# Heads' sums of squares made inside the next unit, and three turns between the load and the rotation of the first queries

## The chip, the core and the metric

One Trainium2 chip, one core. The metric is the device time of one execution in microseconds. Runs of the same kernel agree closely: the three shown lie between 1270.07 and 1270.75 us.

## The reference

One step of a hybrid decoder trunk, for a prompt of 16 meta and 512 new tokens and for 8 sample rows of one token each. All is f32.

```
h = rmsnorm(x) @ w_in;  q, k, v, z_a, u, z_s, g_a, g_s = split(h)
q, k = rope(rmsnorm per head (q, k))          # 16 q heads, 4 kv heads, 64 wide
o_a = sink_attention(q, k, v)                 # window of 128 in blocks of 128, 16 meta keys, one sink per head
      (sample rows: against caches of 16 + 128 keys per row)
y_s = s5_branch(u)                            # diagonal state-space scan, gelu, y * sigmoid(y @ w_glu + b)
out = x + (sigmoid(g_a) * ((o_a * silu(z_a)) @ w_attn_out)
         + sigmoid(g_s) * ((y_s * silu(z_s)) @ w_ssm_out)) @ w_out
```

The per-head rmsnorm needs the sum of squares of each head of q and k: these are "the heads' sums". The kernel also returns the new windows and states.

## The kernel before, in words

**Tiles and units.** Activations lie transposed: features on the 128 partitions, 520 token columns (or 536, with the meta columns) in two column halves of 260 (or 268). Every f32 product is made of three matmuls with split operands (hi x hi, lo x hi, hi x lo). A *unit* is one block of 128 output features: `mm` (L1117) runs over 16 (in later stages 8) blocks of 128 input features and, for each, 3 x 2 matmuls; with 16 that is 96 matmuls in two halves of 48, and ws.get() fetches the weights of each half (`raw` is loaded by SP's queue, ACT makes `whi` at L971, DVE makes `wlo` at L972). After every 24 matmuls `mm` gives the background one step.

**The background** (`Background`, L927) holds three lanes of generators. Each step has a budget; a generator is run until its yielded costs use it up. `yield None` ends its turn for this step. While `fair` is off, as in the attention stage, the first lane that has work is served first and the others get what is left of the step when it yields None.

**Stages.** Some 13 groups of four units in a cheaper scheme ("quads") end at about 374 us. Then the list `ORDER1` runs u units (input of the state-space branch), h units (q, k and v heads) and x units one by one, with the state-space work in the background. Attention follows in the background of the remaining x units (loop at L1616, until nx is 47, and one last unit at L1624 to L1640), of the 8 units of Y1 (the state-space gate) and of the 16 units of Y2. `bg.drain()` (L1670) runs whatever is left, then come the 16 units with A (w_attn_out) and the last quads with w_out.

**Heads' sums.** `heads(i)` (L1283) makes one h unit, scales it and sends it to DRAM. ACT squares it (L1298). Every second unit that is not v closes with four matmuls (L1307) which sum the squares over the 64 features of a head: the stationary operand `k_sel` is 32 columns wide, and the four write four groups of 32 partitions. ACT copies the result (L1310) and two DMAs on SP's queue bring it to skD (k) or sqD (q), L1314. After the last h unit (n is 11) `head_norms()` (L1316) loads these sums, makes inverse roots on DVE and stores them, and the generator `samples()` (sample heads) joins lane 2.

**Attention.** In the generator `attention()` (L1545), values and keys come first, then the sample's attention joins lane 1 (`sample`, L841): 16 pieces of the k cache, each loaded on POOL's queue into one of two `cache` buffers, multiplied with q (L859) and summed (L860) on DVE, later the same for v (L875, L876). Lane 0 goes on with the queries: `load_q` loads raw q rows and their norms on SP's queue, `queries` rotates them on DVE (L650 to L659) and splits them (L727), `blocks` then runs five steps for each of four blocks: `scores` (L743, L744 on PE into the one `aux` bank pair; ACT copies to S, L747; DVE lays the previous block in by a mask, L749), `softmax` (DVE L755, L756, L761, L766; ACT exponentials L759, Pn L765), `turn` (transposes L774, L775; `po` on DVE L778, `pm` and `pp` on ACT L780, L784), `weigh` (L792, DVE L797 into oT). When lanes are empty, `attended` splits oT into A (ACT L1599, DVE L1600), eight pieces.

```
        at.load_q(0)
        yield None
        for kv in range(4):
            yield from at.queries(kv)
            if kv == 0:
                for _ in range(NDELAY):
                    yield None
            yield from at.blocks(kv, kv == 3)
```

Of the kernel before, what the change touches and what calls it, by code (L numbers as in the profile page):

```python
# [897 lines left out]
GBUDGET = 0.4  # L898
BUDGET2, BUDGET3, BUDGET4 = 5.6, 3.0, 4.6
HIGH = 4000  # L900
NDELAY = 2
ATTC = (("kg", 1), ("kgs", 1), ("qg", 1), ("qgs", 1), ("mown", P), ("mprev", P), ("bd64", 4), ("sink", 16))
NXR = 10
# [49 lines left out]
class Stream:  # L953
# [20 lines left out]
    def make(self, i):  # L974
        with self.tc.high_priority(offset=HIGH):
            self.piece(i, self.tiles(i), slice(0, 8))
# [12 lines left out]
class Quads:  # L989
# [29 lines left out]
    def make(self, r):  # L1019
# [9 lines left out]
        lo = pool.tile([P, 8, P], F32R, name="wlo", bufs=bufs)  # L1029
        with self.tc.high_priority(offset=HIGH):  # L1030
            for oi in self.SUMS[s]:
# [20 lines left out]
def trunk(tc, A, O):  # L1052
# [11 lines left out]
    bg = Background(tc)  # L1064
# [34 lines left out]
    def xkeep(kt, src, c):  # L1099
# [14 lines left out]
            v.scalar_tensor_tensor(out=l, in0=s, scalar=g, in1=h.bitcast(F32), op0=ALU.mult, op1=ALU.subtract)  # L1114
        yield

    def mm(n, hi_of, lo_of, w0, budget=None, after=None, pool=None, name=None):  # L1117

        ps = pool.tile([P, 2, 512], F32, name=name) if pool else mmp.tile([P, 2, 512], F32, name="mm")
        W = CH - w0  # L1120
        for h in range(n):
            wh, wl = ws.get()
            for k in range(8):
                kt = 8 * h + k
                first, last = kt == 0, kt == 8 * n - 1
                for (wt, xo, f, l) in ((wh, hi_of, first, False), (wh, lo_of, False, False), (wl, hi_of, False, last)):
                    for c in range(2):
                        m = nc.tensor.matmul(ps[:, c, 0:W], lhsT=wt[:, k], rhs=xo(kt, c), start=f, stop=l)  # L1128
                if k % 4 == 3:
                    bg.last = m.ins  # L1130
                    bg.after = (ws.dve,) if at is not None else ()
                    bg.step((bud[0] if budget is None else budget) / 2)
            if after:
                after(h)
        return ps[:, :, 0:W]
# [147 lines left out]
    def heads(i):  # L1283

        W = CH if i < 4 else 260
        ps = mm_x(CH - W)
        sb = ev.tile([P, 2, W], F32, name="z")
        with tc.high_priority(offset=HIGH):
            v.tensor_tensor(out=sb, in0=ps, in1=R_[:, :, CH - W:], op=ALU.mult)
        nc.sync.dma_start(out=rawD[i][0][:, :, CH - W:], in_=sb)  # L1290
        if i in (2, 3):
            nc.sync.dma_start(out=O["v"][i - 2], in_=sb)
            return
        for q in range(4):
            b = 32 * (q ^ 1)
            nc.sync.dma_start(out=rawD[i][1][b:b + 32, :, CH - W:], in_=sb[32 * q:32 * q + 32])
        sq = ev.tile([P, 2, W], F32, name="t")
        nc.scalar.activation(out=sq, in_=sb, func=AF.Square)  # L1298
        sqs.append(sq)
        if i % 2:  # L1300
            if "ax" not in S:
                S["ax"] = aux.tile([P, 2, 512], F32, name="aux")
            ps = S["ax"][:, 1, P:]
            for c in range(2):
                for j in range(2):
                    o = 64 * j + 32 * c
                    nc.tensor.matmul(ps[o:o + 32, 0:W], lhsT=C["sel"], rhs=sqs[j][:, c], start=True, stop=True)  # L1307
            sqs.clear()
            ss = ev.tile([P, W], F32, name="z")
            nc.scalar.copy(out=ss, in_=ps[:, 0:W])  # L1310
            dst = skD if i < 4 else sqD[2 * (i - 5):2 * (i - 5) + 4]
            dst = dst.rearrange("(j h) (c w) -> j c h w", j=2, c=2)
            for j in range(2):
                nc.sync.dma_start(out=dst[j], in_=ss[64 * j:64 * j + 64:16])  # L1314

    def head_norms():  # L1316
        for src, dst, p, n in ((skD, rkD, 67, 32), (sqD, rqD, P, 65)):
            r1 = ev.tile([p, n], F32, name="z")
            r2 = ev.tile([p, n], F32, name="z")
            flat2 = lambda t: t.rearrange("a b -> (a b)").rearrange("(p n) -> p n", n=n)  # L1320
            nc.sync.dma_start(out=r1, in_=flat2(src))
            v.tensor_scalar(out=r1, in0=r1, scalar1=1.0 / 64, scalar2=1e-6, op0=ALU.mult, op1=ALU.add)
            rsqrt_dve(nc, ev, r2, r1, [p, n], "t", "")
            nc.sync.dma_start(out=flat2(dst), in_=r2)
# [3 lines left out]
    def samples():  # L1328
        smp.extend((yield from sample_heads(nc, sp, dram, smc, C["idn"], rawD, rkD, rqD, S["ax"][:, 1, P:],
                                            lambda: tc.issue_after(bg.last))))  # L1330
# [169 lines left out]
    for n_, (kind, n) in enumerate(ORDER1):  # L1500
# [4 lines left out]
        if kind == "h":  # L1505
            heads(n)
            if n == 11:
                head_norms()
                bg.add(samples(), lane=2)
            continue  # L1510
        if sp is None:
            spool = tc.tile_pool(name="ssm", bufs=2, side="right")
# [25 lines left out]
    def attention():  # L1538
# [32 lines left out]
        at.load_q(0)  # L1571
        yield None
        for kv in range(4):
            yield from at.queries(kv)
            if kv == 0:
                for _ in range(NDELAY):
                    yield None
            yield from at.blocks(kv, kv == 3)
# [313 lines left out]
```

## Time and profile before

| | us |
|---|---|
| runs | 1270.07, 1270.47, 1270.75 (median 1270.47) |
| profiled execution: its time | 1270.79 |
| its span (first to last instruction) | 1268.7 |
| busy: PE | 1257.2 (99%) |
| busy: DVE | 962.5 (76%) |
| busy: ACT | 621.9 (49%) |
| busy: POOL | 262.1 (21%) |
| granted clock of PE, mean | 0.998 |

PE is the engine that sets the time in nearly every stage, so one reads this profile from PE's few gaps: the list of what PE waited for, and the timeline of PE, where each main matmul of 260 columns starts 0.12 us after the one before it. The distance between two starts above that is lost. The other engines matter where PE waits for them. The line numbers are those of the kernel before; in the changed kernel the lines behind the edits stand 1 to 11 lower down (L1128 becomes L1132, L1307 becomes L1313, L1599 and L1600 become L1610 and L1611).

### The profile page before, as it was taken

How to read it: one execution, taken by the hardware profiler on the slowest of the kernel's cores; microseconds unless marked ns; L12 is line 12 of the kernel's file. 1: busy time of each engine (PE TensorE's matmuls, PEld its weight loads, DVE VectorE, ACT ScalarE, POOL GpSimd, SP SyncE). 2: the span in 40 equal slices, each digit the busy share in tenths (PEclk: the TensorE clock that was granted, in tenths of full speed). 3: DMA queues.
4: the chain of work that ended last, by engine and by line, in shares of the span. 5: the costliest groups of instructions: out<-in, count | busy, mean ns of one | idle time of the engine just before them, and what ended most of it. 6: DMA issues, size and time to landing. Idle time of an engine off the chain costs nothing.

```text
span 1268.7 us, 26523 instructions
## 1 busy us (share of the span) xinstructions
PE 1257.2 (99%) x10405; PEld 1231.7 (97%) x10405; DVE 962.5 (76%) x1535; ACT 621.9 (49%) x1330; POOL 262.1 (21%) x434
## 2 busy tenths in 40 slices
PE   9999999999999999999999999999999999999998
PEld 9999999999999999999999999899899999999998
DVE  8686878887785676887668668899876567787875
ACT  8554454454458655445532233576666433344342
POOL 0003999930002222022214131211100000000000
PEclk9999999999999999999999999999999999999999
DMA  8544343353447654555554499677854555565441
GB/s 292 205 160 154 124 142 119 133 168 131 146 133 230 182 163 137 168 164 163 154 151 120 137 283 277 211 239 228 266 167 151 187 183 185 158 202 156 150 138 52
DMA packets 107905, 219.13 MB, mean 173 GB/s; under 512 B 21884, under 2 KB 47444, under 8 KB 107748
## 3 DMA queue, kind: packets, MB, share of 16 engines
q1 hardware_dynamic: 99172, 198.53, 48.8%
q0 software_dynamic: 8608, 18.90, 5.7%
q8 instruction: 82, 1.34, 0.4%
q14 instruction: 43, 0.35, 0.1%
HBM read 181.50 MB, written 36.79 MB: 172 GB/s over the span
## 4 chain that ended last, share of the span: by engine, by line
PE 86%; issue 5%; DMA 4%; DVE 2%; ACT 1%; SPq 1%; POOL 1%; DVEq 0%; POOLq 0%; ACTq 0%
PE mm L1128 44%; PE pr L1335 32%; PE wg L792 2%; DMA xr<-in_x 1%; PE aux L1335 1%; PE aux L1128 1%; PE mm L1637 1%; PE tr L526 1%; PE wg L526 1%; PE aux L743 1%; DMA cache<-in_kc 1%; PE aux L744 1%; PE tr L774 1%; DMA qv<-qD 0%; PE tr L469 0%
## 5 line engine op out<-in xcount | busy, mean ns | idle before, releaser
L1038 DVE TENSOR_TENSOR wlo<-raw,whi 128x1024 fp32r<-128x1024 f32 x147 | 181.7, 1256 | 61.1 <-ACT whi L1037 59.0
L1037 ACT CAST whi<-raw 128x1024 fp32r<-128x1024 f32 x147 | 151.8, 1049 | 147.7 <-DVE raw L1036 68.9
L971 ACT CAST whi<-raw 128x1024 fp32r<-128x1024 f32 (+3 forms) x136 | 130.8, 971 | 169.9 <-PE mm L1128 96.4
L1128 PE MATMUL mm<-xh,whi 128*128 128x260 f32 (+1 forms) x888 | 207.3, 287 | 0.3 <-ACT xr L1186 0.3
L1128 PE MATMUL mm<-xh,wlo 128*128 128x260 f32 (+1 forms) x888 | 205.0, 285 | 0.0
L1128 PE MATMUL mm<-xl,whi 128*128 128x260 f32 (+1 forms) x888 | 204.3, 284 | 0.0
L972 DVE TENSOR_TENSOR wlo<-raw,whi 128x1024 fp32r<-128x1024 f32 (+3 forms) x136 | 152.0, 1125 | 64.5 <-ACT whi L971 64.0
L1335 PE MATMUL pr<-cb,whi 128*128 128x260 f32 x848 | 153.0, 283 | 0.0
L1128 PEld LDWEIGHTS mm<-xh,whi 128*128 128x128 f32 x888 | 147.3, 188 | 4.4 <-issue 2.3
L1128 PEld LDWEIGHTS mm<-xh,wlo 128*128 128x128 f32 x888 | 147.1, 188 | 1.5 <-issue 1.4
L1128 PEld LDWEIGHTS mm<-xl,whi 128*128 128x128 f32 x888 | 147.9, 188 | 0.0
L1335 PE MATMUL pr<-tau,whi 128*128 128x260 f32 x800 | 145.4, 283 | 0.0
L1335 PEld LDWEIGHTS pr<-cb,whi 128*128 128x128 f32 x848 | 130.8, 188 | 0.2 <-ACT z L1369 0.2
L1335 PEld LDWEIGHTS pr<-tau,whi 128*128 128x128 f32 x800 | 123.2, 188 | 0.0
L1335 PE MATMUL pr<-cb,wlo 128*128 128x260 f32 x424 | 119.1, 283 | 0.2 <-DVE wlo L1038 0.2
L1335 PE MATMUL pr<-tau,wlo 128*128 128x260 f32 x400 | 112.9, 282 | 0.0
L1036 DVE TENSOR_TENSOR raw<-raw 128x1024 f32<-128x1024 f32 x83 | 103.9, 1251 | 1.4
L1128 PE MATMUL mm<-Y,whi 128*128 128x260 f32 x576 | 104.6, 287 | 0.0
L1128 PEld LDWEIGHTS mm<-Y,whi 128*128 128x128 f32 x576 | 83.6, 188 | 2.3 <-issue 2.3
L1335 PE MATMUL pr<-xh,wlo 128*128 128x260 f32 x304 | 85.5, 283 | 0.0
L1335 PE MATMUL pr<-xl,whi 128*128 128x260 f32 x304 | 85.5, 283 | 0.0
L1128 PE MATMUL mm<-xhq,whi 128*128 128x260 f32 (+1 forms) x296 | 84.3, 285 | 0.0
(423 smaller groups left out, 2983.9 us busy)
## 6 DMA issues: line engine op xcount, KB each, us to landing
raw<-in_w SPq DMA_DIRECT2D x202, 512.0 KB, 4.4
gD<-z SPq DMA_DIRECT2D x38, 260.0 KB, 4.3
t<-gD SPq DMA_DIRECT2D x32, 260.0 KB, 2.7
cache<-in_vc POOLq DMA_DIRECT2D x16, 286.0 KB, 3.6
cache<-in_kc POOLq DMA_DIRECT2D x15, 288.0 KB, 4.9
xr<-in_x SPq DMA_DIRECT2D x16, 268.0 KB, 6.8
xg<-in_x SPq DMA_DIRECT2D x8, 536.0 KB, 4.2
sbw<-rawD SPq DMA_DIRECT2D x16, 260.0 KB, 7.5
```

Of the source, the lines that this page charges most:

```text
L526: nc.tensor.matmul(o[n], lhsT=D["CL"][:, 2 * e + n, i, 1:5], rhs=H[:, 2 * e + n, i, 0:140], start=False, stop=(i == 1))
L743: nc.tensor.matmul(ps[:, e, 0:272], lhsT=q, rhs=KH[:, k0:k0 + 272], start=True, stop=False)
L744: nc.tensor.matmul(ps[:, e, 0:272], lhsT=q, rhs=KL[:, k0:k0 + 272], start=False, stop=True)
L774: nc.tensor.transpose(out=ps[:, 128 * r:128 * r + 128], in_=Pn[:, r], identity=C["idn"])
L792: nc.tensor.matmul(pv[64 * e:64 * e + 64, 0:256], lhsT=V, rhs=pr[:, e::2], start=(i == 0), stop=(i == len(parts) - 1))
L971: nc.scalar.copy(out=hi, in_=raw)
L972: self.dve = nc.vector.tensor_tensor(out=lo, in0=raw, in1=hi.bitcast(F32), op=ALU.subtract).ins
L1036: nc.vector.tensor_tensor(out=o, in0=o, in1=i, op=ALU.add)
L1037: nc.scalar.copy(out=hi, in_=t)
L1038: nc.vector.tensor_tensor(out=lo, in0=t, in1=hi.bitcast(F32), op=ALU.subtract)
L1128: m = nc.tensor.matmul(ps[:, c, 0:W], lhsT=wt[:, k], rhs=xo(kt, c), start=f, stop=l)
L1335: m = nc.tensor.matmul(bank, lhsT=wt[:, p], rhs=x(p, e), start=first and f and p == 0, stop=l and p == 7, skip_group_check=not first and l ...
```

## The change

Two edits. The four matmuls of the sums, with the copy and the stores behind them, become a function `sums` on a list `pend`. The list is emptied inside `mm`, behind the first half (48 matmuls) of the next unit. The head norms and the start of the sample heads go the same way. And for kv 0, three turns (`NLOAD`) stand between the load of the first q rows and their rotation.

```diff
+NLOAD = 3
...
+    pend = []
+
     def mm(n, hi_of, lo_of, w0, budget=None, after=None, pool=None, name=None):
...
                     bg.step((bud[0] if budget is None else budget) / 2)
+            while pend and h == 0:
+                pend.pop(0)()
             if after:
                 after(h)
...
         sqs.append(sq)
-        if i % 2:
+        def sums():
             if "ax" not in S:
...
                 nc.sync.dma_start(out=dst[j], in_=ss[64 * j:64 * j + 64:16])
+
+        if i % 2:
+            pend.append(sums)
...
             if n == 11:
-                head_norms()
-                bg.add(samples(), lane=2)
+                pend.extend((head_norms, lambda: bg.add(samples(), lane=2)))
...
         for kv in range(4):
+            if kv == 0:
+                for _ in range(NLOAD):
+                    yield None
             yield from at.queries(kv)
```

The scheduler that writes out the order of each engine moves more than the diff shows. Three places:

**The sums, on PE.** The first heads' sums (aux<-t,k_sel). Before, the first matmul stands between the last matmul of the h unit and the next unit:

```order
L1128 MATMUL mm<-xl,whi 128x268 x2
L1128 MATMUL mm<-xh,wlo 128x268 x2
L1307 MATMUL aux<-t,k_sel 32x268
L1128 MATMUL mm<-xh,whi 128x268
L1128 MATMUL mm<-xhq,whi 128x268
```
and the other three 24 matmuls later:

```order
L1128 MATMUL mm<-xh,whi 128x268 x2
L1128 MATMUL mm<-xl,whi 128x268 x2
L1307 MATMUL aux<-t,k_sel 32x268 x3
L1128 MATMUL mm<-xh,wlo 128x268 x2
L1128 MATMUL mm<-xh,whi 128x268
```
In the change they stand together, behind state-space products (tr, wg), half a unit later:

```order
L1132 MATMUL mm<-xl,whi 128x268 x2
L1132 MATMUL mm<-xh,wlo 128x268 x2
L523 MATMUL tr<-U,T 128x140
L523 MATMUL wg<-U,T 128x140
L1313 MATMUL aux<-t,k_sel 32x268 x4
L1132 MATMUL mm<-xh,whi 128x268
L1132 MATMUL mm<-xhq,whi 128x268
```
Of the five sums, the first, second, fourth and fifth now are such a row of four. The third is still one (next to eight small matmuls of L391) and, four main matmuls later, three.

**The k cache pieces and the masks, on DVE.** Before, in the last x unit (L859 and L860 are cache pieces, L749 the mask of a scores bank, L755 the softmax's maximum, L797 the result of a weighing):

```order
L860 TENSOR_REDUCE ssc<-cache 128x9
L859 TENSOR_TENSOR cache<-cache,qv 128x576
L749 COPY_PREDICATED S<-k_attc,aux 128x2x128
L766 TENSOR_TENSOR Pm<-S,den 128x64
L797 TENSOR_TENSOR oT<-wg,zr 128x2x2x32 x2
L860 TENSOR_REDUCE ssc<-cache 128x9
L755 TENSOR_REDUCE m<-S 128x4
L1158 TENSOR_TENSOR z<-mm,R 128x520
L972 TENSOR_TENSOR wlo<-raw,whi 128x1024
L859 TENSOR_TENSOR cache<-cache,qv 128x576
```
In the change, ahead of and at the first split of Y1 (L1611):

```order
L859 TENSOR_TENSOR cache<-cache,qv 128x576
L653 TENSOR_TENSOR sbw<-sbw 128x520
L860 TENSOR_REDUCE ssc<-cache 128x9
L1164 TENSOR_TENSOR z<-mm,R 128x520
L860 TENSOR_REDUCE ssc<-cache 128x9
L973 TENSOR_TENSOR wlo<-raw,whi 128x1024
L659 TENSOR_TENSOR sbw<-sbw,rb 128x4x64 x2
L859 TENSOR_TENSOR cache<-cache,qv 128x576
L860 TENSOR_REDUCE ssc<-cache 128x9
L1611 TENSOR_TENSOR Y1q<-Y1q,Y_10622 128x520
L973 TENSOR_TENSOR wlo<-raw,whi 128x1024
L1611 TENSOR_TENSOR Y_10622<-Y_10622 128x520 x4
```
The last mask ahead of these rows stands 16 rows earlier; from the first scores' mask on, ten L859 stand ahead of the first L1611, with three further masks among the first five. The first L755 comes behind the splits. On PE the scores of (kv 0, block 0) start 73 main matmuls later than before, and the first transposes (tr<-k_idn,Pn) 306 main matmuls later; 312 main matmuls lie between the first scores and the first product with Y1.

**The end of the attention, on PE.** Before, the last weighing (wg) stands 117 main matmuls ahead of the first product with A:

```order
L1128 MATMUL mm<-Y_10774,whi 128x260 x2
L792 MATMUL wg<-po,dV 64x256 x2
L792 MATMUL wg<-pm,Vm 64x256 x2
L1128 MATMUL mm<-Y2q,whi 128x260
L792 MATMUL wg<-pp,V 64x256 x2
L1128 MATMUL mm<-Y2q,whi 128x260
L1128 MATMUL mm<-Y_10774,wlo 128x260 x2
```
In the change it is the drain that issues it, and the products with A follow directly:

```order
L1132 MATMUL mm<-Y_10717,wlo 128x260 x2
L1132 MATMUL mm<-Y_10717,whi 128x260 x2
L1132 MATMUL mm<-Y2q,whi 128x260 x2
L1132 MATMUL mm<-Y_10717,wlo 128x260 x2
L774 MATMUL tr<-k_idn,Pn 128x128
L775 MATMUL wg<-k_idn,Pm 64x128
L774 MATMUL tr<-k_idn,Pn 128x128 x3
L792 MATMUL wg<-po,dV 64x256 x2
L792 MATMUL wg<-pm,Vm 64x256 x2
L792 MATMUL wg<-pp,V 64x256 x2
L1132 MATMUL mm<-A_12807,whi 128x260 x6
L1132 MATMUL mm<-A_12807,wlo 128x260 x2
```
Between the last scores and these transposes stand 33 main matmuls and the weighing of the block before. On DVE the steps behind those last scores stand close to each other (L749, L755, L756, L761, L797 of the block before, L766, the last evacuation of Y2, L778, one weight split, L797, eight L1611); on ACT likewise, with one weight cast ahead of the last `pm`.

## Rows read from the trace of the kernel before

**Rows 1.** The page, part 1: busy time of each engine, its share of the span, and its instructions.
```profile
PE 1257.2 (99%) x10405; PEld 1231.7 (97%) x10405; DVE 962.5 (76%) x1535; ACT 621.9 (49%) x1330; POOL 262.1 (21%) x434
```

**Rows 2.** What PE waited for, over the whole span: the waiting operation and line, the engine and line that ended the wait, us in total, number of times, the longest.
```profile
PE aux L743 <- DVE S L749: 2.2, 2, 2.0
...
PE wg L792 <- ACT pp L784: 0.7, 1, 0.7
...
PE tr L526 <- DVE H L512: 0.6, 1, 0.6
PE aux L743 <- DVE m L756: 0.5, 1, 0.5
```

**Rows 3.** Timeline of PE around the first two parts of one heads' sums (start us, duration us, engine, line, operation, out<-in, shapes, count; the profiler has two records for each matmul of the sums).
```profile
437.30 0.41 PE L1128 MATMUL mm<-xh,wlo 128*128 128x268 f32 x2
437.63 0.64 PE L1307 MATMUL aux<-t,k_sel 128*32 128x268 f32 x2
438.20 0.39 PE L1128 MATMUL mm<-xh,whi 128*128 128x268 f32 x1
438.43 0.28 PE L1128 MATMUL mm<-xhq,whi 128*128 128x268 f32 x1
...
442.26 0.40 PE L1128 MATMUL mm<-xl,whi 128*128 128x268 f32 x2
442.59 0.65 PE L1307 MATMUL aux<-t,k_sel 128*32 128x268 f32 x6
443.18 0.51 PE L1128 MATMUL mm<-xh,wlo 128*128 128x268 f32 x2
```

**Rows 4.** Timeline of PE around the longest wait of the attention stage (the idle time before an instruction and what ended it stand in brackets).
```profile
809.90 0.28 PE L1628 MATMUL mm<-xlq,whi 128*128 128x260 f32 x1
812.14 0.39 PE L743 MATMUL aux<-KH,QT 128*128 128x272 f32 x1 [1.96 <-DVE S L749]
...
813.34 0.81 PE L1628 MATMUL mm<-xl,whi 128*128 128x260 f32 x3
...
816.76 0.42 PE L1628 MATMUL mm<-xl,whi 128*128 128x260 f32 x2
```

**Rows 5.** Windows of 1 us behind that wait: busy us (and instructions) of PE, PE's weight loads, DVE, ACT and POOL, then the granted clock of PE, the DMA share and GB/s.
```profile
815.00:816.00 1.00, 1.00 (x7) 1.00 (x6) 1.00 (x2) 0.97 (x3) 0.00 (x0) 0.50 0.69 230
...
817.00:818.00 1.00, 1.00 (x11) 1.00 (x10) 0.94 (x2) 1.00 (x7) 0.00 (x0) 1.00 1.02 322
```

**Rows 6.** Timeline of DVE in the same place.
```profile
807.12 0.72 DVE L860 TENSOR_REDUCE ssc<-cache 128x9 f32<-128x576 f32 x1
810.97 0.76 DVE L859 TENSOR_TENSOR cache<-cache,qv 128x576 f32<-128x576 f32 x1 [3.13 <-DMA cache<-in_kc]
811.65 0.44 DVE L749 COPY_PREDICATED S<-k_attc,aux 128x256 f32<-128x256 int32 x1
```

**Rows 7.** The tile that the sample's cache pieces are loaded into: time from a load's issue to its landing.
```profile
DMA to landing us min/median/max: 3.0/4.3/9.3
```

**Rows 8.** Windows of 25 us, columns as in the windows above.
```profile
860.00:885.00 25.00, 25.00 (x207) 23.52 (x207) 24.71 (x45) 16.09 (x44) 3.17 (x6) 1.00 0.77 229
885.00:910.00 25.00, 23.43 (x191) 22.03 (x191) 22.82 (x41) 13.99 (x37) 5.12 (x9) 1.00 0.77 243
960.00:985.00 25.00, 25.00 (x205) 22.70 (x205) 13.98 (x29) 16.02 (x51) 0.19 (x1) 1.00 0.43 148
```

**Rows 9.** Timeline of ACT from the last scores of the attention to the split of A.
```profile
981.07 0.40 ACT L747 COPY S<-aux 128x288 f32<-128x288 f32 x1
...
984.07 0.41 ACT L759 ACTIVATE S<-S,m 128x145 f32<-128x145 f32 x1
...
986.95 1.28 ACT L765 ACTIVATE Pn<-S,den 128x128 f32<-128x128 f32 x4 [1.17 <-DVE den L761]
990.15 1.12 ACT L780 ACTIVATE pm<-wg,k_attc 64x128 f32<-64x128 f32 x4 [1.91 <-PE wg L775]
...
992.11 0.59 ACT L784 COPY pp<-tr 128x512 f32<-128x512 f32 x1
997.00 4.32 ACT L1599 CAST A<-oT 128x520 fp32r<-128x520 f32 x8 [4.31 <-DVE oT L797]
```

**Rows 10.** Timeline of DVE in the same stretch.
```profile
982.06 0.76 DVE L755 TENSOR_REDUCE m<-S 128x4 f32<-128x580 f32 x1
...
985.62 1.22 DVE L972 TENSOR_TENSOR wlo<-raw,whi 128x1024 fp32r<-128x1024 f32 x1
...
996.36 0.49 DVE L797 TENSOR_TENSOR oT<-wg,zr 128x128 f32<-128x128 f32 x2 [2.73 <-PE wg L792]
997.66 0.70 DVE L1600 TENSOR_TENSOR A<-oT,A 128x520 fp32r<-128x520 f32 x1 [0.81 <-ACT A L1599]
```

**Rows 11.** Timeline of PE in the same stretch, and its first product with A.
```profile
980.74 0.29 PE L744 MATMUL aux<-KL,QT 128*128 128x272 f32 x1
...
995.66 0.65 PE L792 MATMUL wg<-pp,V 128*64 128x256 f32 x4
996.24 0.38 PE L1128 MATMUL mm<-Y2q,whi 128*128 128x260 f32 x1
...
1010.35 0.64 PE L1128 MATMUL mm<-A,whi 128*128 128x260 f32 x4
```

## The prediction

> **What bounds the kernel now.** I read the page first: TensorE (PE) is busy for 1257.2 of 1268.7 us [rows 1], so time can come only from its few gaps or from work on PE that costs more than its matmuls. Next the list of what PE waited for. Its rows for the attention stage are the ones this change can touch: the scores L743 behind the masking copy L749 with 2.2 us in two waits, one of them 2.0 us, the scores behind the softmax's L756 with 0.5, the weighing L792 behind pp with 0.7, and, in the state-space part, L526 behind H with 0.6 [rows 2]. Then the timeline of PE around the heads' sums, for what one batch of sums costs [rows 3]; PE, the clock and DVE around the long wait at 809.9 us [rows 4 to 6]; the cache pieces' landing times [rows 7]; the share of DVE in the later stages [rows 8]; and, for the end of the attention, the chain from the last scores to the first product of the attention's output on ACT, DVE and PE [rows 9 to 11]. All sums are made against the profiled execution, 1270.79 us (its span of 1268.7 and 2.1 around it); the median of the three runs is 1270.47, 0.32 below.
>
> **The sums' merge.** Nothing is added or removed: 20 matmuls in five heads' sums stay. Before, one of each four is issued at once and three a step later; the order of the change has four batches of four, and one batch (the third) still as one and three. So ten batches become six. A batch's price is read from PE's starts. The main matmuls follow each other every 0.12 us. From 437.30 two of them run, the next was due at 437.55; it starts at 438.20, and its follower 0.23 instead of 0.12 later: 0.65 + 0.11 = 0.76 us for a batch of one (two records) [rows 3]. For three (six records) it is 442.26 to 443.18 less 0.25, so 0.67, and about 0.1 again: 0.77. One and three cost the same, so I price four the same. Four batches fewer are 4 x 0.76 = **-3.0 us**. All of this lies on PE's path. The lower bound of the gain is 2.2: one batch in four stood beside another interruption, where it is worth less.
>
> The sums' results come later by up to half a unit (48 matmuls, 5.8 us). Behind them hang ACT's copy, two DMAs each on SP's queue, and for the last batch the head norms on DVE with loads and stores in SP's queue. On DVE these norms now stand ahead of the state-space step H and of an evacuation. The wait for H of 0.6 [rows 2] is of this kind; I expect it to remain and charge **+0.5** for a second one like it, between 0 and 2.5 (the largest wait of the whole list is 2.0).
>
> **The three turns.** They move the first q rows' scores by 73 matmuls, and give the background's turns to the sample lane. In the old order, the L749 at 811.65 stood behind the multiply L859 of a cache piece; DVE stood still for 3.13 us until that piece had landed [rows 6], and PE, in front of the next scores, from 809.90 to 812.14 [rows 4]. DVE takes its instructions in order, so the L749, whose own data was ready, waited for a DMA that it does not need. In the new order this stretch of DVE holds cache pieces, then the splits L1611 of Y1, with no L749 between them; PE has no scores there. The first transposes move by some 300 matmuls. I take the waits of L749 and L756 as gone: 2.2 + 0.5 = **-2.7**. After the long wait the granted clock fell to 0.50, the 1.2 GHz level, and was back at 1.00 by 817 [rows 5]. Between 813.34 and 816.76 [rows 4] lie 16 matmuls, 0.214 us each instead of 0.12: 16 x 0.094 = **-1.5**.
>
> What is late next? The rule that hurt there still holds: the pieces land 3.0 to 9.3 us after issue, median 4.3 [rows 7], and two buffers feed them. From the first scores on, ten pieces now lie ahead of Y1's splits, with three L749 among the first five. With 4.3 us to land and 1.5 us of DVE work, two buffers give a piece each 2.9 us, 29 us in all, against the 312 matmuls of 0.12 us, 37 us, that PE has from those scores to its first product with Y1; that is room for one landing of 9 us, not for two. Behind it the attention of the prompt, which was spread from 788 us on, must be done in about 1000 matmuls instead of 1200. DVE was busy 24.71 and 22.82 of 25 us in 860 to 910, but only 13.98 in 960 to 985 [rows 8]; the work is pushed towards the slack, but through the full stretch. For pieces and packing together I charge **+1.0**, between 0 and 4.0 (two waits like the one that goes).
>
> **The tail.** Before, the last weighing began at 995.66 and the first product with A ran at 1010.35 [rows 11]: 14 us of Y2 products covered the split of A. In the new order the last block is still open when those products end, and its transposes, its weighing and the A products stand directly behind each other. So part of the chain shows. In the old run it is: last scores start at 980.74, S copied, masked, maximum done by 982.82; the exponentials begin only at 984.07, normalising Pn ends at 988.23 (986.95 + 1.28); transposes, po and pm and pp (990.15 to 992.70); weighing (the last third 995.66 to 996.31); oT at 996.36, splits from 997.00 on ACT, first low half done on DVE at 998.36 [rows 9 to 11]. From the end of the scores at 981.03 this is 17.3 us, but it holds places where the chain stood behind other work. Without the 1.25 us before the exponentials and the 1.22 us of a weight split L972 on DVE [rows 10], the softmax takes 7.2 - 2.5 = 4.7 us. PE has as cover 33 matmuls (4.0 us) and the weighing of the block before (three thirds of 0.58, 1.7): 5.7. So the transposes are not late. Then pm (1.12) and pp (0.59) follow on ACT, 1.7 us, of which the parts of the weighing that need them late leave PE idle for about 1.2; after the weighing oT, the first high and the first low half take from 996.31 to 998.36, 2.0 us. Together **+3.2**. The low end is 2.0, if only the last step shows. The high end is 5.5: the softmax at its old pace is 1.5 late (7.2 - 5.7), and a weight cast between pm and pp, as in the old run, adds 0.84 (992.11 less 991.27).
>
> The 2.0 us wait at 809.9 was followed by a stretch at the low clock [rows 4, 5]; the 1.57 us that PE lost in parts between 885 and 910 were not, the clock stayed at 1.00 [rows 8]. The tail has two waits of 1 to 2 us with a weighing between. I take no low clock, and keep 1.5 for the bound. The Trainium skill's "TensorE: Matmul & The Clock Gate" (Part 1, What's actually happening) says that an idle TensorE drops to 1.2 GHz and must be busy again before it gets 2.4 GHz back. By that rule, which speaks against an open end of the attention, the two waits would cost those 1.5 us too, and the sum would be -1.0 instead of -2.5.
>
> **Sum:** -3.0 + 0.5 - 2.7 - 1.5 + 1.0 + 3.2 = -2.5 us; against the median 1270.47 that is **1268.0**.
>
> **The rivals.**
> - **The tail shows in full (slower).** If the chain keeps its old 17.3 us and PE has for it only the cover of 5.7, the weighing of 1.7 and five transposes (0.6 at 0.12 each), 9.3 us are idle instead of 3.2, and the clock falls: -2.5 + 6.1 + 1.5 = +5.1, so 1275.6. It decides from 6.7 us of idle time on (with the low clock behind them, -2.5 + 3.5 + 1.5 = +2.5). For it: ACT and DVE take the chain in order between weight casts and splits. Against it: nothing but one cast and one split of weights lies in the new order between those steps, and of the 17.3 us 3.0 were PE's own order (pp was ready at 992.70, its weighing began at 995.66). Chance 0.17.
> - **The wait moves (same).** A piece that lands late holds up L749 in the few scores left, or Y1's splits: then the 4.2 of the kv 0 stretch come back as another wait of 2 us with its low clock. -2.5 + 3.5 = +1.0, so 1271.5. For it: the last scores ahead of Y1 stand between pieces in the same pattern as at 809.9 (two L859 between two L749). Chance 0.22.
> - **All of it hidden (faster).** No new waits ahead, a tail of 2.0: -7.2 + 2.0 = -5.2, so 1265.3. For it: DVE's slack at 960 to 985 [rows 8]. Chance 0.20.
> - **The turns do nothing** but move the scores, and a wait like that at 809.9 stays: -3.0 + 0.5 + 3.2 = +0.7, so 1271.2. DVE's rotation of q stands at nearly the same place of its order as before, which speaks for it; the missing L749 there speaks against. Chance 0.05.
>
> **How the numbers follow.** My own case has 0.36, from 1266.5 to 1269.5, and its middle stands right at the bound of 0.2% (2.5 us), about what a measurement of this kernel can tell from no change. Faster: 0.20 of the hidden case, and 0.20 of mine and its neighbours: 0.40. Slower: the full tail with 0.17. The rest, 0.43, is no difference. The range leaves out the outer half of the hidden case and the outer half of the full tail: 1264.5 to 1274.0.
>
> **What would show it.** Right: sums in batches of eight records with gaps of 0.8; no wait for L749 over 1 us near 790 to 812 and no low clock there; a wait of the last weighing for pm or pp and of the first A product for its splits near 1005, 2 to 6 us together. Wrong: a low clock behind that tail, PE waiting over 2 us for Y1's splits or for H, or batches that cost by their number of matmuls.

## The result, and the profile after

The change is slower: 1276.38 us (median of 8 runs, 1273.15 to 1280.88) against 1270.61 of the kernel before (8 runs, 1269.23 to 1273.25). The ratio is 1.0044, 95% interval 1.0026 to 1.0061, so +5.6 us between +3.3 and +7.8. The forecast was 1268.0, with a range to 1274.0; both the sign and the range missed.

The profiled execution took 1280.88 us (span 1279.1), the longest of its eight; the one of before took 1270.79, close to its median. The 10.4 us between the two spans therefore hold some 4.5 us that a middling execution doesn't have. TensorE (PE) is busy for 1258.9 us, 1.7 more than before [rows 1]: most of the time lost is waits, not work. (In the rows DVE is VectorE, ACT is ScalarE, POOL is GpSimd and SP is SyncE.)

What PE waited for in the changed kernel (columns as in [rows 2]):

```profile
PE tr L526 <- DVE H L512: 3.4, 1, 3.4
PE mm L1132 <- ACT Y L1610: 2.3, 1, 2.3
PE mm L1132 <- ACT A L1610: 1.5, 1, 1.5
PE wg L792 <- ACT pm L780: 1.4, 1, 1.4
PE wg L710 <- DVE mt L703: 1.1, 1, 1.1
...
PE mm L1132 <- DVE Y2q L1611: 0.9, 1, 0.9
PE tr L709 <- issue: 0.8, 1, 0.8
PE wg L792 <- DVE po L778: 0.8, 1, 0.8
PE wg L775 <- DVE Pm L766: 0.7, 1, 0.7
...
PE aux L391 <- ACT z L1316: 0.4, 1, 0.4
...
PE aux L743 <- DVE S L749: 0.3, 1, 0.3
```

The two L743 waits of 2.2 and 0.5 us [rows 2] are gone but for 0.3. The wait for H, 0.6 before, is 3.4. The splits of Y1, of one Y2 piece and of A (L1610, L1611), never waited for before, are waited for now, and so is po; pm, 0.3 us before, is 1.4.

To see where time is lost, take the same main product (a matmul of 260 or 268 columns; both kernels have 9480, counted from the start) in both traces and subtract its start times:

| main product | before, us | after less before, us | between this row and the one above |
|---|---|---|---|
| 3300 | 406.60 | -0.08 | |
| 5100 | 669.34 | -2.53 | the five sums |
| 5250 | 690.98 | +2.00 | the wait for H, low clock |
| 6000 | 790.67 | +4.10 | waits in the values' transposes (L709, L710) |
| 6450 | 863.39 | -6.11 | scores come later, no kv 0 waits; Y1 waits here |
| 7200 | 987.69 | -1.84 | waits at Y2q, po, Pm; postponed matmuls |
| 7500 | 1026.21 | +10.38 | the rest of the postponed matmuls, the tail |

The -6.11 is mostly a debt: the attention's own matmuls were moved behind product 6450, and were done by 7500.

A batch of sums in the changed kernel, on PE (columns as in [rows 3]):

```profile
443.65 0.40 PE L523 MATMUL wg<-U,T 128*128 128x140 f32 x2
443.99 0.66 PE L1313 MATMUL aux<-t,k_sel 128*32 128x268 f32 x8
444.57 0.39 PE L1132 MATMUL mm<-xh,whi 128*128 128x268 f32 x1
```

Eight records take 0.66 us, what two took in [rows 3]: four matmuls of 32 columns in four column groups cost what one does.

The wait for H, on PE, and what DVE did ahead of it, first in the kernel before:

```profile
681.20 0.51 PE L526 MATMUL tr<-H,CL 128*128 128x140 f32 x2 [0.58 <-DVE H L512]
```
```profile
661.65 0.31 DVE L587 TENSOR_SCALAR qs<-x,k_smc 128x64 f32<-128x64 f32 x1
...
663.69 0.42 DVE L483 TENSOR_TENSOR p<-tr,tab 128x264 f32<-128x264 f32 x1
...
680.72 0.42 DVE L512 TENSOR_TENSOR H<-rt,rt 128x264 f32<-128x264 f32 x1
```

Then in the changed kernel:

```profile
677.34 0.28 PE L1132 MATMUL mm<-xh,whi 128*128 128x260 f32 x1
681.06 0.51 PE L526 MATMUL tr<-H,CL 128*128 128x140 f32 x2 [3.44 <-DVE H L512]
```
```profile
663.58 0.31 DVE L587 TENSOR_SCALAR qs<-x,k_smc 128x64 f32<-128x64 f32 x1 [4.27 <-DMA x<-rawD]
...
664.08 0.43 DVE L483 TENSOR_TENSOR p<-tr,tab 128x264 f32<-128x264 f32 x1
...
676.25 0.18 DVE L562 TENSOR_TENSOR t<-z 67x32 f32<-67x32 f32 x1
...
680.47 0.20 DVE L1331 TENSOR_SCALAR z<-z 128x65 f32<-128x65 f32 x1 [1.29 <-DMA z<-sqD]
680.58 0.43 DVE L512 TENSOR_TENSOR H<-rt,rt 128x264 f32<-128x264 f32 x1
```

DVE stands still twice on the way to H. First 4.27 us in front of L587, the sample heads, for the load x<-rawD, with the state-space step L483 queued behind it. Its matmuls (L469) had already been issued from 657.61 on. Then 1.29 us in front of L1331, the q head norms, for z<-sqD, with H queued behind. SP issued that load only at 676.46:

```profile
656.73 0.24 SPq L1330 DMA_DIRECT2D z<-skD  x1
...
659.33 1.11 SPq L1320 DMA_DIRECT2D sqD<-z  x2
670.59 5.43 SPq L971 DMA_DIRECT2D raw<-in_w  x2
676.46 0.33 SPq L1330 DMA_DIRECT2D z<-sqD  x1
```

H itself came no later than before: L512 ran at 680.58 against 680.72. PE's wait grew by 2.9 us because PE was there that much earlier, so the lead of the sums was given back, and a stretch at the low clock came on top.

The end of the attention on PE, which answers to [rows 11]:

```profile
1015.59 0.49 PE L774 MATMUL tr<-k_idn,Pn 128*128 128x128 f32 x3
1017.45 0.65 PE L792 MATMUL wg<-po,dV 128*64 128x256 f32 x4 [1.37 <-ACT pm L780]
...
1018.37 0.60 PE L792 MATMUL wg<-pp,V 128*64 128x256 f32 x4
1020.45 1.19 PE L1132 MATMUL mm<-A,whi 128*128 128x260 f32 x6 [1.49 <-ACT A L1610]
```

Windows of the changed kernel (columns as in [rows 5]); before, only the stretch of [rows 5] had a low clock in the places that the change touches:

```profile
680.00:685.00 5.00, 3.94 (x19) 3.94 (x20) 4.44 (x8) 0.78 (x3) 2.39 (x4) 0.67 0.18 24
...
825.00:830.00 5.00, 5.00 (x31) 5.00 (x30) 4.83 (x8) 3.89 (x6) 0.00 (x0) 0.66 1.01 312
...
900.00:905.00 5.00, 4.98 (x27) 4.00 (x28) 5.00 (x9) 2.55 (x10) 0.00 (x0) 0.66 0.86 268
...
1020.00:1025.00 5.00, 4.55 (x36) 4.40 (x37) 4.61 (x8) 4.05 (x8) 0.00 (x0) 1.00 0.63 224
```

Each of the three windows with a mean of 0.66 or 0.67 holds a stretch at 0.50, the 1.2 GHz level. These stretches stand behind the waits for H, for Y1's splits, and for Y2q and po. Behind the tail there is none.

### The profile page after: what moved, and what is told of

The parts are those of the page before. It is cut to its first block, busy times and chain, and to the rows that moved or that the text cites. A ratio compares the mean times of both kernels' runs of the same rounds, so it can differ in the third digit from the quotient of the medians.

```text
span 1279.1 us, 26547 instructions
## 1 busy us (share of the span) xinstructions
PE 1258.9 (98%) x10405; PEld 1234.2 (96%) x10405; DVE 963.8 (75%) x1535; ACT 621.1 (49%) x1330; POOL 261.7 (20%) x434
## 4 chain that ended last, share of the span: by engine, by line
PE 81%; DVE 5%; issue 5%; DMA 4%; ACT 3%; SPq 1%; POOL 1%; DVEq 0%; POOLq 0%; ACTq 0%
PE mm L1132 41%; PE pr L1344 32%; PE wg L792 1%; PE aux L1344 1%; PE aux L1132 1%; DMA cache<-in_kc 1%; ACT whi L972 1%; DVE wlo L973 1%; PE tr L526 1%; PE wg L526 1%; PE aux L743 1%; DMA Y<-yD 1%; DMA t<-yD 1%; PE aux L744 0%; ACT xh L1112 0%
## 5 line engine op out<-in xcount | busy, mean ns | idle before, releaser
L1132 PE MATMUL mm<-Y,whi 128*128 128x260 f32 x576 | 107.7, 291 | 2.5 <-ACT Y L1610 2.3
```

## The experiments

All were timed in five rounds beside the kernel before, whose median was 1269.7 to 1270.6 us in these sets. Ratios are to it, with the 95% interval. Unless said otherwise an edit is made to the changed kernel.

### First: which half costs, and is it the queue?

**e1**, the sums alone (`NLOAD = 0`). 

> The sums' merge alone, without the three turns. Theory (queue): the merge gives 2.9 us back, but the load of the q sums stands behind two weight loads in SP's queue and comes some 13 us later, so PE waits about 3 us for H near 680 us and runs a stretch at the low clock after it (1.5): +1 to +2 over the kernel before, 1272. Rival (turns): all of the loss comes from the three turns; the merge alone gains 2.9, 1267.7, and the wait for H stays near 0.6.

**e2**, the three turns alone: `sums()` runs at once, in the old place, and so do the head norms.

```diff
-        def sums():
+        if i % 2:
...
-                pend.extend((head_norms, lambda: bg.add(samples(), lane=2)))
+                head_norms(); bg.add(samples(), lane=2)
```


> The three turns alone, with the sums as before. Theory (lost cover): the waits at 790 to 812 go (-4.2 with their low clock), but PE waits 2 to 3 us for Y1's splits near 822, with a low clock after it, 2 to 3 us among the packed attention near 897, and 2.5 to 3.5 us at the end of the attention: +3 to +5, 1274 to 1275.5. Rival (sums): the turns are neutral or gain and the loss is the sums' alone: 1268 to 1271.

**e3**, the head norms' loads on ACT's queue, past the weight loads of SP.

```diff
-            nc.sync.dma_start(out=r1, in_=flat2(src))
+            nc.scalar.dma_start(out=r1, in_=flat2(src))
```


> The whole change, but the two loads of the head norms are issued from ACT's queue and not from SP's, where they stand behind weight loads. Theory (queue): the load of the q sums is issued some 7 us earlier, the wait for H near 680 falls from 3.4 to under 0.8 and no low clock follows: 4 us less than the change, 1272. Rival (DVE): H is late because DVE is full of norms and state-space work from 665 to 681; then the wait stays at 2 to 3.4 us and the time near 1276.

**e4**, the last sums, the head norms and the sample heads at once, as before; four merged batches of sums stay.

```diff
-        if i % 2:
+        if i == 11:
+            sums()
+        elif i % 2:
             pend.append(sums)
...
-                pend.extend((head_norms, lambda: bg.add(samples(), lane=2)))
+                head_norms()
+                bg.add(samples(), lane=2)
```


> The whole change, but the last of the five sums and the head norms are made at once, as before. Theory (queue): the load of the q sums stands ahead of the two weight loads again, the wait for H is under 0.8 as in the kernel before; one merge less (+0.8): 3 to 4 us under the change, 1272.5 to 1273.5. Rival (DVE or turns): no difference from the change beyond 0.8 us, 1276 to 1277.

| | median, us | ratio | waits of PE, us |
|---|---|---|---|
| e1 sums only | 1272.59 | 1.0024 [1.0013, 1.0036] | H 3.0 |
| e2 turns only | 1271.38 | 1.0018 [1.0007, 1.0028] | first scores 1.5 and 0.9; tail 1.37 and 1.48 |
| e3 loads on ACT | 1276.89 | 1.0053 [1.0034, 1.0072] | H 3.5 |
| e4 last sums at once | 1273.17 | 1.0031 [1.0016, 1.0045] | H 1.2; first scores 1.5 and 0.9; tail 1.4 and 1.5 |

Both halves are slower and they add up: 3.0 + 2.3 = 5.3 of the 5.6 us. e3 fells the theory of SP's queue: on ACT's queue the load of sqD was issued at 676.73, no earlier. It waits for its target: `r1` is a tile named "z" in a pool with two buffers for that name, and the one it gets is free only after the last read of the k norms' `r1`. That read is L562 in the third Newton step, which ran from 676.25 to 676.43 above; the load followed at 676.46. In e3:

```profile
676.51 0.18 DVE L562 TENSOR_TENSOR t<-z 67x32 f32<-67x32 f32 x1
```
```profile
676.73 0.36 ACTq L1330 DMA_DIRECT2D z<-sqD  x1
```

In the kernel before, e1 and e4, too, this load was issued 0.02 to 0.03 us after the same L562 had ended.

### Second: the shared buffer, and fewer turns

**e5**, buffers of its own for `r1`, three turns; **e8**, the same without turns.

```diff
-            r1 = ev.tile([p, n], F32, name="z")
+            r1 = sp.tile([p, n], F32, name=f"r1_{n}", bufs=1)
```


> The whole change, but the tiles that the head norms load into (r1) have buffers of their own. Theory (buffer): the load of the q sums waits for the k norms' last use of the shared z buffer on DVE (which runs between state-space steps up to 676 us); with a buffer of its own it lands before 672, DVE no longer stands still ahead of H, PE's wait for H falls from 3.4 to under 0.8 with no low clock behind it: 3 to 5 us less than the change, 1271 to 1273. Rival (DVE): the wait stays at 2 to 3 us, because DVE has too much to do from 664 to 681: 1275 to 1277.

> The sums' merge without the turns, and the head norms with buffers of their own. Theory (buffer): the wait for H is under 0.8, and the merge keeps its 2 to 3 us less what L391 waits for the sums' copy (0.5): 1.5 to 2.5 under the kernel before, 1267.5 to 1268.5. Rival (DVE): as the merge alone, 1272.

**e6**, the kernel before with two turns (`NLOAD = 2`), and **e7**, with three and one turn less behind the rotation (`NLOAD = 3`, `NDELAY = 1`).

> The kernel before with two turns in place of the three, sums as before. Theory (edge): the third turn pushes the first softmax's transposes past the last x unit, which gives the background no turns, so that the block loses some 300 matmuls; with two turns the first transposes stand at 5993 instead of 6369 main matmuls and the last weighing again 118 ahead of the first product with A: no wait at the end of the attention, 1.5 to 4 us less than with three turns, 1267.5 to 1270. Rival (each turn has its price): a wait of 1 to 2 us at the end and 1270.5 to 1271.5.

> The kernel before with the three turns, and one instead of two turns of delay behind the rotation of the first queries (NDELAY 1). The last weighing stands 34 main matmuls (4 us) ahead of the first product with A. Theory (edge): the wait for A's split goes and that for pm too (under 0.5 together), 1268 to 1270.5. Rival (the loss comes from packing, not from the end): 1271 to 1273 with waits of over 2 us in the middle of the attention.

| | median, us | ratio | waits of PE, us |
|---|---|---|---|
| e5 own buffers | 1274.41 | 1.0047 [1.0032, 1.0062] | H 1.2; first scores 2.7, low clock behind |
| e8 sums, own buffers | 1270.23 | 1.0003 [0.9993, 1.0014] | H 1.9; QT 3.5 |
| e6 two turns only | 1268.04 | 0.9993 [0.998, 1.0006] | no tail; QT 1.0, L1679 0.9 |
| e7 three turns, one delay | 1269.57 | 0.9996 [0.9985, 1.0007] | no tail; H 0.5, first scores 1.2 and 0.9 |

The buffer is a part of it: without turns the sums cost +0.4 us instead of +3.0, though the wait for H is 1.9 still. With three turns, e5, they gained nothing that can be told (+6.0 us by its ratio, against +5.6): the wait for H fell, and PE waited 2.7 us in front of the first scores instead. e6 and e7 have no tail: the last weighing stands 118 main products ahead of A in e6 and 34 in e7, against none in the changed kernel. The third turn, with two behind the rotation, is what puts the last block against A. By their ratios e6 and e7 are at -0.9 and -0.5 us, neither to be told from no change, and 2.8 to 3.2 us below e2, about as much as e2's tail of 2.85.

### Third: combinations

**e9**, the sums as in e4 without turns; **e10**, the change with two turns; **e11**, that with own buffers; **e12**, e9 with two turns. The edits are those above.

> The first four sums merged into the next unit, the last sums and the head norms as before, no turns. Theory (buffer): the gain of three merged batches, 2.3 less about 0.5 for L391 behind the sums' copy, comes through because H is not later than before: 1 to 2 under the kernel before. Rival (a moved batch costs as much as it saves): no difference, within 0.6 of it.

> The whole change with two turns instead of three. Theory (edge for the turns, buffer for the sums, and the two add up): the merge's +3.0 stays and the turns' +2.3 becomes -0.9, so +1 to +3 over the kernel before, with no wait at the end of the attention and the wait for H near 3. Rival (the two edits work on each other): over +4, as with three turns.

> The whole change with two turns and with the head norms' load tiles in buffers of their own. Theory (edge and buffer add up): +0.4 of the merge with such buffers and -0.9 of two turns: -2 to +1 against the kernel before, no wait at the end, a wait for H of 1 to 2. Rival: the time of the change, +4 and more.

> The first four sums merged, the last as before, two turns. Theory (edge and buffer): -1.5 of the four sums and -0.9 of the two turns: 1.5 to 3.5 under the kernel before, which would beat both kernels. Rival: within 1 of the kernel before, since what PE saves ahead of 740 us it waits for at the first scores near 780.

| | median, us | ratio | wait for H, us |
|---|---|---|---|
| e9 | 1270.66 | 1.0006 [0.9995, 1.0017] | 1.5 |
| e10 | 1273.33 | 1.0029 [1.0016, 1.0043] | 2.7 |
| e11 | 1270.81 | 1.0008 [0.9996, 1.002] | 1.9 |
| e12 | 1269.03 | 0.9999 [0.9987, 1.001] | 2.4 |

None beats the kernel before. Own buffers take off as much with two turns (e10 to e11) as with none (e1 to e8), 2.7 us by the ratios. Every kernel with the merge keeps a wait for H of 1.2 us or more, own buffers or not.

### Fourth: what is left of the wait for H

**e13**, e8 without the three Newton steps of the head norms; **e14**, the same with three turns. Both leave work out, so their norms are only rough; they are there for what the work on DVE costs.

```diff
-            rsqrt_dve(nc, ev, r2, r1, [p, n], "t", "")
+            rsqrt_dve(nc, ev, r2, r1, [p, n], "t", "", iters=0)
```


> As e8 (sums merged, norm tiles of their own, no turns), and the head norms leave out their three Newton steps (18 small DVE operations, 3.6 us; the roots are then only rough). Theory (DVE is full ahead of H): the wait for H falls under 0.8 and the merge's gain comes out: 2 to 3 us less than e8, 1267.5 to 1268.5. Rival (H's own chain of PE, DVE and DMA sets it): the wait stays at 1 to 2 us and the time within 1 us of e8.

> The whole change with norm tiles of their own and without the Newton steps of the head norms. Theory (the two edits add up): the turns' +2.3 alone, less 0 to 2 of the merge: 1270 to 1272.5 beside 1274.4 of e5. Rival: 1274 to 1276, as e5, because what is saved at H is waited for at the first scores near 780.

e13: 1269.28, ratio 0.9995 [0.9983, 1.0007]; the wait for H stays, 1.6 us. e14: 1272.39, 1.0014 [0.9999, 1.0028]; H 1.8. So DVE's extra steps are not what holds H. e13's trace shows the other stand-still, in front of L587: 5.35 us.

**e15** takes that away: e8 with the sample heads' nine products (L587 to L592) on POOL. **e16** is e15 with two turns, **e17** the kernel before with this edit alone, **e18** e15 with three turns.

```diff
-        v.tensor_scalar(out=dst, in0=x[:, bl], scalar1=smc[:, n:n + 1], scalar2=smc[:, 4:5], op0=ALU.mult, op1=ALU.mult)
+        nc.gpsimd.tensor_scalar(out=dst, in0=x[:, bl], scalar1=smc[:, n:n + 1], scalar2=smc[:, 4:5], op0=ALU.mult, op1=ALU.mult)
...
-    v.tensor_copy(out=kvs[:, 2:4], in_=x[:, 2:4])
+    nc.gpsimd.tensor_copy(out=kvs[:, 2:4], in_=x[:, 2:4])
```


> The sums' merge with own buffers for the head norms and no turns (as in e8), and the nine products of the sample heads (L587 to L592) on GpSimd instead of VectorE. Theory, DVE stands in line: in e8 VectorE stood 3.57 us in front of L587 for the load x<-rawD, with the state-space step L483 behind it, whose matmuls had long been done, so the wait for H of 1.95 is the merge's lead given back. Without L587 on VectorE that idle time goes, L483 starts 2 us or more earlier, the wait for H is under 0.5, no low clock at 680 to 685, and the main product 5250 comes 2 us or more ahead of where it is in the kernel before; time 1267.5 to 1269. Rival, PE's lead is lost at H for another reason (the scan chain of VectorE is as long as the lead): the wait stays over 1.0, time as e8, 1270.

> As e15, with two turns. If the two cures add to the two turns (which alone gave 0.9993), 1266 to 1267.5, the first kernel that beats the one before; if the attention gives the lead back at its first scores, as in e8 and e9, 1269 to 1270.

> The kernel before, with the sample heads' nine products on GpSimd and nothing else. In the kernel before VectorE did not wait in front of L587, so this should change nothing by itself: 1270.0 to 1270.8, with the wait for H at 0.6 or less. If it is faster by over 2 us, what e15 gains is not the merge's.

> The whole change with three turns, own buffers for the head norms and the sample heads on GpSimd. The wait for H should go (under 0.5), and what is left against the kernel before is the turns' own +2.3 less the merge's 2: 1270 to 1271. If the wait for H goes and the time stays at 1274, the lead is given back in the attention.

| | median, us | ratio | wait for H, us |
|---|---|---|---|
| e15 sums, own buffers, POOL | 1267.88 | 0.9982 [0.997, 0.9994] | 0.5 |
| e16 with two turns | 1265.21 | 0.9959 [0.9944, 0.9974] | 0.2 |
| e17 before, POOL only | 1270.14 | 0.9994 [0.9984, 1.0005] | under 0.2 |
| e18 with three turns | 1271.79 | 1.0011 [1.0, 1.0023] | 0.5 |

DVE and POOL in e15:

```profile
660.23 0.42 DVE L483 TENSOR_TENSOR p<-tr,tab 128x264 f32<-128x264 f32 x1
...
677.65 0.42 DVE L512 TENSOR_TENSOR H<-rt,rt 128x264 f32<-128x264 f32 x1
```
```profile
663.88 0.39 POOL L587 TENSOR_SCALAR qs<-x,k_smc 128x64 f32<-128x64 f32 x1 [2.86 <-DMA x<-rawD]
```
```profile
678.13 0.51 PE L526 MATMUL tr<-H,CL 128*128 128x140 f32 x2 [0.50 <-DVE H L512]
```

POOL waits for the load now, L483 starts at 660.23 instead of 664.08, and H comes 2.93 us earlier than in the changed kernel. Product 5250 is 1.99 us ahead of before, and 7500 still 2.63. The control e17 can't be told from the kernel before, so most of the gain in e15 belongs to the merge; how much is not exact, since the intervals of e15 and e17 overlap (up to 0.9994, and from 0.9984). With two turns the medians give 5.4 us less than before, the best of the kernels tried (5.2 by the ratio, 2.0 more than those of e15 and e6 add up to). With three turns e18 is back above e15, at +1.4 us: the two cures take 4.2 us off the change.

## Why the prediction was wrong

**The sums' merge, -3.0: right.** Between products 3300 and 5100 the changed kernel gains 2.45 us and pays 0.37 in a new wait of L391 for the sums' copy; together 2.8. In e15 it is 2.44 and 0.4, in e13 1.94 and 0.95: 2.8 to 2.9 each time, and one, three and four matmuls cost the same.

**"The wait for H ... I expect it to remain and charge +0.5 for a second one like it": this step failed.** It named the place and the cover, the head norms ahead of H on DVE, but sized the wait by the row of before, 0.6 us. Measured: 3.4 instead of 0.6, and a stretch at 0.50 behind it. From product 5100 to 5250 the sign turned, -2.53 to +2.00, 4.5 us: 2.9 of added wait, and about 1.5 for the stretch, as the prediction prices one. The sum let all but 0.5 us of the sums' lead pass H; H was no earlier than before, and none of the lead passed. Two things were left out, and the runs show both. First, a load into a tile of a shared pool waits for the tile's last reader. The norms' step was moved with its DMAs, and I followed their queue, not their buffer; own buffers alone take the sums from +3.0 to +0.4. Second, time gained on PE ahead of a step that stands behind a DMA is not kept: PE came to L469 2.5 us earlier (657.61 against 660.14), but x<-rawD was issued at 655.48 instead of 653.62, L587 ran at 663.58 instead of 661.65, and L483 behind it on DVE began at 664.08 against 663.69. That the sample heads start half a unit later does not explain it: in e4 they start at once, as before, and the load came no earlier; in both kernels POOL waited for the stores of the raw rows (rawD<-z) to land. POOL in the kernel before, the changed kernel and e4, then DVE in e4:

```profile
653.62 1.04 POOL L575 DMA_DIRECT2D x<-rawD  x1 [19.72 <-issue]
```
```profile
655.48 1.04 POOL L575 DMA_DIRECT2D x<-rawD  x1 [23.57 <-DMA rawD<-z]
```
```profile
655.75 1.04 POOL L575 DMA_DIRECT2D x<-rawD  x1 [24.63 <-DMA rawD<-z]
```
```profile
662.83 0.31 DVE L587 TENSOR_SCALAR qs<-x,k_smc 128x64 f32<-128x64 f32 x1 [2.36 <-DMA x<-rawD]
```

e13 and e15 together show that this, too, is the order on DVE and not the length of its work: with the Newton steps gone the wait for H is still 1.6 us, with L587 gone from DVE's path it is 0.5. With both cured the sums give what was forecast for the merge and the H wait together: -2.5 forecast, -2.3 (-3.8 to -0.8) in e15, of which 0.8 may be POOL's own (e17).

**The kv 0 waits, -2.7, and their low clock, -1.5: a second step that failed in part.** The waits left their place: between 790 and 820 us the changed kernel has 0.3 us of L743, and the clock there is 1.00. But the term held nothing for what takes their place at the first scores. In e2, without the merge, PE waits 1.47 and 0.92 there, and 0.56 and 0.32 for later scores: 3.3 us instead of 2.7, without a low clock.

```profile
780.65 0.40 PE L743 MATMUL aux<-KH,QT 128*128 128x272 f32 x1 [1.47 <-ACT S L747]
...
782.93 0.39 PE L743 MATMUL aux<-KH,QT 128*128 128x272 f32 x1 [0.92 <-DVE QT L727]
```

Some 15 us ahead of them DVE had stood 3.26 us for raw q rows, and was busy nearly without a gap from there to QT; that this is what made QT late is read from the order on DVE, and no run takes it away:

```profile
765.81 0.76 DVE L651 SCALAR_TENSOR_TENSOR sbw<-sbw,k_attc 128x520 f32<-128x520 f32 x1 [3.26 <-DMA sbw<-rawD]
```

In the changed kernel's own profile, where PE comes some 4 us later (product 6000), that place is free, and the wait is at Y1's splits, 2.29 us, from the landing of Y<-yD. PE, then ACT:

```profile
823.82 0.51 PE L1132 MATMUL mm<-Y,whi 128*128 128x260 f32 x2 [2.29 <-ACT Y L1610]
```
```profile
823.14 1.80 ACT L1610 CAST Y<-Y 128x520 fp32r<-128x520 f32 x3 [4.58 <-DMA Y<-yD]
```

Everything of the turns but the tail was forecast at -2.7 - 1.5 + 1.0 = -3.2 us. It measured -0.9 and -0.5 in the nearest kernels without a tail, e6 and e7, and about -0.5 in e2 (+2.3 less 2.85).

**Pieces and packing, +1.0: too small in the changed kernel.** The upper bound, 4.0, allowed two waits like the one that goes. The profile has Y1 2.5 (2.29 and 0.23), then 2.4 between 896 and 901 (Pm, Y2q, po), and two stretches at 0.50: by the prediction's 1.5 for such a stretch, 7.9 us. This is the slowest of the eight executions; in e3 and e5, with the same order there, Y1's first wait was 1.72 and 0.80. The rival "the wait moves" came near in size: by its 3.5 the turns alone would cost 3.5, and e2 measured +2.3 (0.9 to 3.6). But it had a cache piece come late, and what came late was Y in the changed kernel and the raw q rows in e2.

**The tail, +3.2: right.** 1.37 for pm and 1.49 for the first split of A, 2.86 together; 1.37 and 1.48 in e2 to e5 and in e14. The slower rival, the tail in full with 6.7 us of idle time and more, did not happen: the kernel was slower by another way. Where the last block keeps main products between itself and A (e6, e7), the tail is not there at all.

**No low clock behind the tail: right**, the clock is 1.00 from 1015 to 1030. The Trainium skill's "TensorE: Matmul & The Clock Gate" (Part 1, What's actually happening) has the clock set by how busy TensorE has been recently, with 1.2 GHz for an idle one. The waits of 3.44 and 2.29, with a stretch at 0.50 behind each, agree with it. The prediction applied it as if any idle time were enough; the tail's 1.37 and 1.49, and a wait of 2.62 in e9, with the clock at 1.00 behind them, show that it is not.

**The sum** was wrong by 5.5 us in the sums' half (-2.5 forecast, +3.0 measured) and by 2.3 in the turns' half (0.0 forecast). The terms that were counted from the trace, the batches and the tail, hold within 0.4 us. The two that were given a round charge for what is late next, +0.5 and +1.0, failed, and so did the -2.7, which took a wait as gone and none as new.

**What stays open.** Executions of one kernel differ by 4 to 11 us between its fastest and slowest (e16 from 1264.18 to 1267.96, e6 from 1264.54 to 1275.13). The kernel before does so too, from 1267.86 to 1275.37 in the last set; that the three runs shown at the start lie so close is chance, and a single profile is not a median. The waits are read from one profile each, and in the traces the place of the waits differs with the landing of loads: e8 and e9 waited 3.5 and 2.6 us for QT, behind a stand-still of DVE of 2.68 and 2.63 us in front of L651 for raw q rows, 0.24 in the kernel before. Which landings are late in which execution was not settled. What holds the stores of the raw rows, and with them x<-rawD, was not tested. Why the third turn costs more than its tail of 2.9 us in e18 against e16 (6.6 us between the medians) was not taken apart either, nor why e16 gains more than e15 and e6 together.

## What to carry to other kernels

When an edit gives one engine a lead, follow that lead to the next place where another engine hands it work, and ask whether that engine starts by the lead or by a DMA: here DVE stood in front of a load with the main chain queued behind it, and moving those few instructions to an idle engine made the merge worth its 2.3 us. When a step with loads is moved, look for the buffer that each load lands in and its last reader, not only for the queue. When work is pushed towards the end of a stage, keep other products between its last piece and the first use.

## What the runs showed of the hardware

Nearly the same idle time gave two clocks. e2 waited 1.47 and 0.92 us in front of the first scores and stayed at full clock; e4, another kernel, waited 1.51 and 0.93 at the same place and fell to 0.50. Windows of 2 us from 782 us on, first e2, whose second wait ends at 782.93, then e4, where it ends at 781.66 (columns as in [rows 5]):

```profile
782.00:784.00 2.00, 1.08 (x9) 1.07 (x9) 1.94 (x4) 0.00 (x0) 0.54 (x1) 1.00 0.85 273
784.00:786.00 2.00, 2.00 (x19) 2.00 (x18) 1.97 (x4) 0.52 (x1) 0.54 (x1) 1.00 0.89 228
```
```profile
782.00:784.00 2.00, 2.00 (x10) 2.00 (x10) 1.97 (x4) 0.00 (x0) 0.14 (x1) 0.50 0.84 247
784.00:786.00 2.00, 2.00 (x14) 2.00 (x14) 1.79 (x3) 0.92 (x2) 0.40 (x1) 0.75 0.98 327
```

So the length of a wait alone does not tell whether the clock falls. Over all kernels here, between 640 and 1040 us, single waits of 1.72 and 1.95 (e3, e8), 1.96 (before), 2.05 and 2.37 (e12) and 2.29 (changed) were followed by a stretch at 0.50, and waits of 1.83 (e14, e11), 1.86 and 1.97 (e11), 1.89 (e10), 2.37 (e16) and 2.62 (e9) were not; the six between 2.67 and 3.55 all were. The tail's pair of 1.4 and 1.5 never was, in seven kernels.

POOL took longer than DVE for the sample heads' products (L587 0.39 us in e15 against 0.31 in the changed kernel, L588 0.84 against 0.31, the first L590 0.83 against 0.17; spans on POOL are rough). Neither this nor its stand-still of 2.86 us for x<-rawD showed in PE's waits.
